# A transformer layer on one core: the first slots of the first stage in an order written out by hand, biases by two-row DMAs, identity products in TensorE's pauses

## The chip, the core and the metric

The kernel runs on one core of one Trainium2 chip. A core has TensorE (PE in the profile, PEld its weight loads), VectorE (DVE), ScalarE (ACT), GpSimd (POOL) and the sync engine (SP), which here only issues DMAs. Each engine works through its own queue in order; they meet through semaphores. Matrix products go to PSUM, which PE fills and DVE and ACT read. The metric is the time of one execution in device microseconds, as the median of several.

## The reference

One layer with a bidirectional retention branch, a grouped attention branch and a squared-ReLU MLP, on 2048 rows of width 1024 and 256 context rows. What the change touches is its beginning:

```python
mod = (c_act @ w_mod + b_mod)[:, None, :]
mod_c = (cc_act @ w_mod + b_mod)[None, None, :]
sh1, sc1, g1, sh2, sc2, g2 = jnp.split(mod, 6, axis=-1)
...
h = _modulate(_rmsnorm(x, norm1_g), sh1, sc1)        # h * (1 + scale) + shift
hc = _modulate(_rmsnorm(xc, norm1_g), csh1, csc1)
rq, rk, rv, rg, aq, ak, av = jnp.split(h @ w_in, SPLIT_IDX, axis=-1)
...
crk, crv = jnp.split(hc @ w_in[:, RK_OFF:RG_OFF], 2, axis=-1)
```

Then come rotary embedding, retention, attention over context and latent keys, the output product, the MLP and a last norm, all in float32.

## The kernel before

The layer runs in stages: the input projections (up to about 600 us), attention, the output product and the MLP. The projections are done in two groups of row tiles of 128: first the two context tiles c0, c1 with the latent tiles l0 to l3, then the other twelve. For each group the columns of `w_in` come in blocks, and a block of one tile is a *unit* or slot. Units follow one another on PE, and `run_step(s)` issues what else is due at unit s: loads, roundings of weights, evacuations, rotary embedding, stores. The table `do(s, part, fn)` is filled ahead with these, at distances in slots written out by hand. Engines see their instructions in the order in which the program issues them.

To keep float32 accuracy a product runs as three: the operand and the weights are each split into a rounded part (`hi`, by ACT) and the rest (`lo`, by DVE), and hi*hi, hi*lo and lo*hi are summed in one PSUM bank. That is the trio L1186, L1187 and L1188 of `products`.

The first block, the retention keys of the first six tiles (tiles 0 to 5 are c0, c1, l0 to l3), can't begin before the scale and shift of the norm are known, and these need the modulation. The function `start` therefore weaves both. Width 1024 is cut into quarters q of 256 columns. `Modulation(q)` loads its part of `w_mod` in four pieces (L340, two DMAs each), multiplies it on PE (L350, `product`), adds the bias (`end`, L353), turns the columns with an identity on PE (`columns`, L301) and takes sums to the shift `s1` and the scale `a1` (`shift_and_scale`, L360 to L363). `Rows` loads a tile of x, squares it (ACT, L460), takes the inverse root (POOL, L464 and L465) and scales the rows (DVE `norm`, L469); before, tiles go in pairs here. `Part(q, tile)` turns two 128-wide pieces of a tile (PE, L483), scales them (DVE, L488), adds the shift (POOL, L492), rounds (ACT `high`, L495) and takes the rest (DVE `low`, L498). `Weight` fetches and splits a quarter's two rows of key weights (L520, L526, L535).

*Round* q means the products of quarter q for tiles 0 to 4 (six a tile, `begun[n]` is the tile's bank); tile 5 has no bank until the end and runs all four quarters at once. Rounds 0 to 2 also carry the modulation of the next quarter. The list `order` in `start` is the order of the loads on the sync queue; `ahead` issues the next ones when one of six staging buffers (`wst`) has become free. Biases go out on ACT's queue, 32 rows of the same values each.

PSUM pools: `psM` one bank for the modulation's sums, `psT` two for turns, `psO` five for products.

Of the kernel before, what the change touches and what calls it, by code (L numbers as in the profile page):

```python
# [22 lines left out]
P = 128  # L23
# [33 lines left out]
def layer_kernel(ctx: ExitStack, tc: tile.TileContext, a: dict, out: bass.AP):  # L57
# [215 lines left out]
    with ExitStack() as st, tc.manual_schedule():  # L273
# [45 lines left out]
        class Modulation:  # L319
# [186 lines left out]
        class Weight:  # L506
# [8 lines left out]
            def fetch(self, j):  # L515
# [4 lines left out]
                nc.sync.dma_start(w, src.rearrange("(k p) n -> p k n", p=P))  # L520

# [679 lines left out]
        for (g, col), w in weights.items():  # L1201
# [93 lines left out]
        def start():  # L1295

            G, w0 = GROUPS[0], weights[0, C_RK]
            rows_ = mq.tile([P, 512], F32, name="mb", tag="mb", bufs=2)
            mods = [Modulation(q, rows_) for q in range(4)]
            rows = Rows(G, 2)  # L1300
            begun = {}
            for n in range(6):
                hs[0, n] = new_h(0, *G[n])
            order = [("m", 0, 0), ("x", 0), ("m", 0, 2), ("m", 0, 4), ("x", 1), ("m", 0, 6)]
            order += [("w", 0), ("x", 2), ("x", 3), ("m", 1, 0), ("x", 4), ("m", 1, 2), ("x", 5)]
            order += [("m", 1, 4), ("m", 1, 6), ("w", 1)]
            for q in (2, 3):
                order += [("m", q, k) for k in range(0, KT, 2)] + [("w", q)]
            room = [6]

            def ahead(n=1):
                room[0] += n
                while order and (order[0][0] == "x" or room[0]):
                    what, *at = order.pop(0)
                    if what == "x":
                        rows.load(*at)
                    elif what == "m":
                        room[0] -= 1
                        mods[at[0]].load(at[1])
                    else:  # L1320
                        room[0] -= 1
                        w0.fetch(*at)

            for m in mods[:2]:
                m.bias()
            nc.sync.dma_start(n1, a["n1"])
            ahead(0)

            def settle(*ns):
                for n in ns:  # L1330
                    rows.square(n)
                rows.root()
                for n in ns:
                    rows.norm(n)

            for k in range(0, KT, 2):
                mods[0].product(k)
                ahead()
            settle(0, 1)
            mods[0].end()  # L1340
            mods[0].shift_and_scale()
            w0.high(0)
            w0.low(0)
            ahead()
            parts = {}

            def begin(q, n):
                if q < 4 and n < 6:
                    p = parts[q, n] = Part(G[n][0], rows.x[n], hs[0, n], 2 * q, 2)
                    p.turn()  # L1350
                    p.scale()
                    p.shift()

            begin(0, 0)
            begin(0, 1)
            for q in range(4):
                for n in range(6):
                    parts[q, n].high()
                    parts[q, n].low()
                    if q == 0 and n == 2:  # L1360
                        settle(4, 5)
                    if q > 0 or n > 1:
                        begin(q, n + 2)
                    if n < 5:
                        if q == 0:
                            begun[n] = psO.tile([P, 512], F32, name="pso", tag="pso")
                        products(begun[n], hs[0, n], w0, 512, range(2 * q, 2 * q + 2))
                    elif q == 3:
# [1035 lines left out]
```

## Time and profile before

| | |
|---|---|
| time, median of 3 runs | 2692.89 us (2688.63 to 2694.88) |
| the profiled execution | 2693.04 us, span 2691.2 us, granted clock 0.997 |
| PE busy | 2618.1 us, 97% of the span |
| DVE, ACT, POOL busy | 2034.9, 1526.6 and 1729.1 us |
| first key product | 20.71 us |
| last product of the key block issued | 87.24 us |

A timeline row gives start, length, engine, line, instruction, what it writes and reads, how many were merged (x2), and in brackets how long the engine was idle before it and what ended that. Instructions on an engine are pipelined: a product of 0.39 us can follow another after 0.23. A float32 product that is not a turn has two records, so x16 of L350 are eight products. Names leave tile numbers out (`hhi_c` is the rounded part of c0 or c1). A row of a stretch gives the busy time of each engine in it.

### The profile page before, as it was taken

How to read it: one execution, taken by the hardware profiler on the slowest of the kernel's cores; microseconds unless marked ns; L12 is line 12 of the kernel's file. 1: busy time of each engine (PE TensorE's matmuls, PEld its weight loads, DVE VectorE, ACT ScalarE, POOL GpSimd, SP SyncE). 2: the span in 40 equal slices, each digit the busy share in tenths (PEclk: the TensorE clock that was granted, in tenths of full speed). 3: DMA queues.
4: the chain of work that ended last, by engine and by line, in shares of the span. 5: the costliest groups of instructions: out<-in, count | busy, mean ns of one | idle time of the engine just before them, and what ended most of it. 6: DMA issues, size and time to landing. Idle time of an engine off the chain costs nothing.

```text
span 2691.2 us, 45667 instructions
## 1 busy us (share of the span) xinstructions
PE 2618.1 (97%) x16759; PEld 1469.3 (55%) x16759; DVE 2034.9 (76%) x3032; ACT 1526.6 (57%) x2572; POOL 1729.1 (64%) x1351
## 2 busy tenths in 40 slices
PE   6999999998999999999999899999999999999998
PEld 3876555546666666666666444444444444444443
DVE  3688798677888888888887497989877566556686
ACT  2756444325877778788878576666666322222243
POOL 2545466545666668787787595777663566666686
PEclk9999999999999999999999999999999999999999
DMA  6766999746022113323332565666694857574453
GB/s 231 253 229 194 312 321 333 251 140 214 28 75 68 54 54 113 92 81 90 88 107 73 215 193 157 225 214 218 223 317 133 289 174 276 176 297 160 169 179 119
DMA packets 325065, 480.02 MB, mean 178 GB/s; under 512 B 82148, under 2 KB 192228, under 8 KB 320360
## 3 DMA queue, kind: packets, MB, share of 16 engines
q1 hardware_dynamic: 324456, 476.84, 53.4%
q8 instruction: 132, 2.16, 0.3%
q14 instruction: 93, 0.76, 0.1%
q10 hardware_dynamic: 384, 0.26, 0.0%
HBM read 320.03 MB, written 156.38 MB: 177 GB/s over the span
## 4 chain that ended last, share of the span: by engine, by line
PE 82%; DVE 8%; DMA 4%; ACT 3%; issue 2%; POOL 0%; SPq 0%; DVEq 0%; ACTq 0%; POOLq 0%
PE pd L2217 7%; PE pd L2216 7%; PE pd L2215 7%; PE pu L1988 7%; PE pu L1989 7%; PE pu L1990 7%; PE o L248 4%; PE st L214 4%; PE st L215 4%; PE pso L1188 4%; PE pso L1186 3%; PE pso L1187 3%; PE mp L177 3%; PE o L247 2%; PE bank L1757 2%; PE bank L1755 2%
## 5 line engine op out<-in xcount | busy, mean ns | idle before, releaser
L190 DVE TENSOR_REDUCE nm<-mp 128x1 f32<-128x512 f32 x558 | 379.2, 685 | 118.8 <-PE mp L177 103.6
L231 POOL TENSOR_TENSOR plo<-p,phi 128x1024 f16<-128x1024 f32 x160 | 346.1, 2164 | 157.5 <-ACT phi L224 136.0
L220 ACT ACTIVATE p<-st 128x512 f32<-128x512 f32 x576 | 340.4, 597 | 141.2 <-PE st L215 131.3
L1988 PE MATMUL pu<-hf,w1f 128*128 128x512 f16 x896 | 340.0, 379 | 0.0
L1989 PE MATMUL pu<-hf,w1f 128*128 128x512 f16 x896 | 339.8, 379 | 0.0
L1990 PE MATMUL pu<-hf,w1f 128*128 128x512 f16 x896 | 339.8, 379 | 0.0
L2215 PE MATMUL pd<-w,uf 128*128 128x512 f16 x896 | 339.6, 379 | 0.0
L2216 PE MATMUL pd<-w,uf 128*128 128x512 f16 x896 | 339.6, 379 | 0.0
L2217 PE MATMUL pd<-w,uf 128*128 128x512 f16 x896 | 339.6, 379 | 0.0
L2235 POOL TENSOR_TENSOR y<-y,d 128x512 f32<-128x512 f32 x128 | 210.4, 1646 | 147.5 <-ACT uf L2204 95.3
L224 ACT ACTIVATE phi<-p 128x1024 f16<-128x1024 f32 x288 | 303.8, 1055 | 0.0
L233 DVE TENSOR_TENSOR plo<-p,phi 128x512 f16<-128x512 f32 x256 | 235.9, 923 | 19.6 <-ACT phi L224 7.8
L248 PE MATMUL o<-wv,phi 128*128 128x129 f16 x2304 | 240.7, 220 | 0.0
L214 PE MATMUL st<-qr,ks 128*128 128x512 f16 x576 | 218.6, 380 | 14.9 <-ACT p L220 14.8
L247 PE MATMUL o<-wv,plo 128*128 128x65 f16 x2304 | 233.0, 193 | 0.0
L247 PEld LDWEIGHTS <-plo 128*128 128x128 f16 x2304 | 208.0, 98 | 22.0 <-issue 0.6
L215 PE MATMUL st<-qr,ks 128*128 128x512 f16 x576 | 218.5, 379 | 0.0
L248 PEld LDWEIGHTS <-phi 128*128 128x128 f16 x2304 | 205.2, 97 | 23.4
L2227 DVE SCALAR_TENSOR_TENSOR y<-pd,scy,y 128x512 f32<-128x512 f32 x160 | 116.9, 747 | 131.8 <-PE pd L2217 131.5
L2000 DVE TENSOR_TENSOR r<-pu,r 128x512 f32<-128x512 f32 x224 | 149.9, 684 | 83.3 <-PE pu L1990 59.5
L1186 PE MATMUL pso<-wf,h_l 128*128 128x512 f16 (+1 forms) x576 | 208.2, 361 | 0.0
L1188 PE MATMUL pso<-wf,h_l 128*128 128x512 f16 (+1 forms) x576 | 208.1, 361 | 0.0
(374 smaller groups left out, 6124.2 us busy)
## 6 DMA issues: line engine op xcount, KB each, us to landing
wm<-in_w_ff SPq DMA_DIRECT2D x64, 512.0 KB, 7.1
u<-r SPq DMA_DIRECT2D x128, 256.0 KB, 4.3
ur<-u SPq DMA_DIRECT2D x128, 256.0 KB, 5.5
y<-x SPq DMA_DIRECT2D x64, 512.0 KB, 6.9
wf<-w2f SPq DMA_DIRECT2D x112, 256.0 KB, 3.0
w<-wf SPq DMA_DIRECT2D x28, 1024.0 KB, 9.3
w1r<-in_w_ff SPq DMA_DIRECT2D x48, 512.0 KB, 4.9
x<-y SPq DMA_DIRECT2D x48, 512.0 KB, 2.9
```

Source lines behind the costliest of these rows:

```text
L190: nc.vector.tensor_reduce(dst, src, axis=AX.X, op=ALU.max, negate=True)
L214: mm(ps, ks[:, self.g, k], q[:, 0], start=True, stop=False)
L220: nc.scalar.activation(self.p[kt // 2][:, kt % 2], self.s.pop(kt), AF.Exp, scale=HD**-0.5)
L231: nc.gpsimd.tensor_tensor(lo, p, hi, op=ALU.subtract)
L247: mm(o[:, : HD + 1], lo[:, i, c], v[:, : HD + 1], start=False, stop=False)
L248: mm(o, hi[:, i, c], v[:, :VW], start=False, stop=last)
L1988: mm(pu[hf, i], whi, hi, start=k == 0, stop=False)
L1989: mm(pu[hf, i], whi, lo, start=False, stop=False)
L1990: mm(pu[hf, i], wlo, hi, start=False, stop=k == 3)
L2215: mm(ps, u[:, 0, b], w[:, b, 0], start=b == 0, stop=False)
L2216: mm(ps, u[:, 0, b], w[:, b, 1], start=False, stop=False)
L2217: mm(ps, u[:, 1, b], w[:, b, 0], start=False, stop=b == 3)
```

## The change

All in the first stage, in `start` and what it calls:

- Tiles are normed one by one (`Rows([t], 1)`), and the loads are ordered anew: the last modulation piece of quarter 0 ahead of tile 1, weights of quarters 2 and 3 ahead of the last piece of their modulation.
- The order of the first slots is written out. In round 0 each slot has the hi products of a tile, the turn and scaling of the next, the square and norm of the one after it, then the lo products and a piece of the next modulation. From the last tile of round 0 on, a slot has the hi products of its tile (`hi`, L1366 in the rows below), turns listed in `turns` for later slots, the split of what the slot before turned (`split_part`), and the lo products of the slot before (`lo`, L1371). A tile's `run_step` comes one slot later.
- `keep_on(n)` issues n products of the identity with itself (L1340) into the bank of tile 4 before that bank is used.
- Biases are two rows of each 32 (rows 0 and 16, the only ones that are read), in a buffer that POOL clears once at the start; those of quarters 2 and 3 go out on the sync queue.
- Weights of this block are split in two halves (`high_row`, `low_row`), and the columns are turned in the bank of `psM`.
- The weights of the attention queries (`C_AQ`) of the first group are fetched two slots and rounded one slot earlier.

The core of the diff:

```diff
-            def bias(self):
-                nc.gpsimd.memset(self.b[64:], 0.0)
+            def bias(self, queue):
...
-                    nc.scalar.dma_start(self.b[32 * i : 32 * i + 32], src.partition_broadcast(32))
+                    queue.dma_start(self.b[32 * i : 32 * i + 32 : 16], src.partition_broadcast(2))
...
-                ps = columns(self.b, 2, psT.tile([P, 4, P], F32, name="psx", tag="psx"))
+                ps = columns(self.b, 2, psM.tile([P, 4, P], F32, name="mps", tag="mps"))
...
+            def high_row(self, j, r):
...
+                nc.scalar.activation(self.w[j][0][:, r], self.raw[j][:, r], AF.Copy)
...
+                if (g, col) == (0, C_AQ):
+                    f, h = s - 7 + j, s - 4 + j
...
-            order = [("m", 0, 0), ("x", 0), ("m", 0, 2), ("m", 0, 4), ("x", 1), ("m", 0, 6)]
-            order += [("w", 0), ("x", 2), ("x", 3), ("m", 1, 0), ("x", 4), ("m", 1, 2), ("x", 5)]
-            order += [("m", 1, 4), ("m", 1, 6), ("w", 1)]
+            order = [("m", 0, 0), ("x", 0), ("m", 0, 2), ("m", 0, 4), ("m", 0, 6), ("w", 0), ("x", 1), ("x", 2)]
+            order += [("m", 1, 0), ("x", 3), ("m", 1, 2), ("x", 4), ("m", 1, 4), ("m", 1, 6), ("w", 1), ("x", 5)]
             for q in (2, 3):
-                order += [("m", q, k) for k in range(0, KT, 2)] + [("w", q)]
+                order += [("m", q, 0), ("m", q, 2), ("m", q, 4), ("w", q), ("m", q, 6)]
...
+            def keep_on(n):
+                for _ in range(n):
+                    mm(bank_of(4)[:, :P], ident, ident, start=True, stop=True)
...
+            keep_on(5)
+            add(0, 0)
+            square(0)
+            rows[0].norm(0)
+            keep_on(3)
+            add(0, 2)
+            keep_on(1)
+            add(0, 4)
+            turn(0, 0)
+            add(0, 6)
+            mods[0].end()
+            for r in range(2):
+                w0.high_row(0, r)
+            keep_on(1)
+            settled(0)
+            scale(0, 0)
+            for r in range(2):
+                w0.low_row(0, r)
...
+            keep_on(3)
+            parts[0, 0].high()
+            square(1)
+            parts[0, 0].low()
+            rows[1].norm(0)
+            for n in range(4):
+                hi(0, n)
+                if n == 0:
+                    keep_on(4)
+                turn(0, n + 1)
+                scale(0, n + 1)
+                if n < 3:
+                    square(n + 2)
+                parts[0, n + 1].high()
+                if n < 3:
+                    rows[n + 2].norm(0)
+                parts[0, n + 1].low()
+                lo(0, n)
+                add(1, 2 * n)
+                if n < 2:
+                    mods[2 + n].bias(nc.sync)
+                keep_on(2)
+            mods[1].end()
+            turn(1, 0)
+            settled(1)
+            scale(1, 0)
+            waiting = [(1, 0)]
+            turns = {(0, 4): [(1, 1), (1, 2)], (2, 2): [(0, 5), (1, 5)], (3, 2): [(2, 5)], (3, 3): [(3, 5)]}
+            for q in (1, 2, 3):
+                turns[q, 0], turns[q, 1] = [(q, 3)], [(q, 4)]
+                if q < 3:
+                    turns[q, 3], turns[q, 4] = [(q + 1, 0), (q + 1, 1)], [(q + 1, 2)]
+            pieces = {0: (0,), 1: (2,), 2: (4, 6)}
+            slots = [(0, 4)] + [(q, n) for q in (1, 2, 3) for n in range(5)]
+            for i, (q, n) in enumerate(slots):
+                ready, waiting = waiting, []
...
+                hi(q, n)
+                if n == 3 and q < 3:
+                    mods[q + 1].end()
+                    settled(q + 1)
+                for p in turns.get((q, n), ()):
+                    turn(*p)
+                    scale(*p)
+                    waiting.append(p)
+                for p in ready:
+                    split_part(*p)
...
+                if i:
+                    lo(*slots[i - 1])
+                if q in (1, 2):
+                    add(q + 1, *pieces.get(n, ()))
```

What this makes of PE's queue around the first key products. The names are `mps` for the modulation's bank, `psx` for turns, `pso` for a tile's bank, `x_c0` for tile 0 and so on, `hhi` and `hlo` for a part's rounded and remaining half; numbers are buffers. Before, from the last modulation piece of quarter 0:

```order
L350 MATMUL mps_393<-wst_379,cst_337 32x256 x4
L301 MATMUL psx_436<-ident_60,mb_346 128x128 x2
L483 MATMUL psx_449<-ident_60,x_c0_369 128x128 x2
L483 MATMUL psx_454<-ident_60,x_c1_377 128x128 x2
L1186 MATMUL pso_461<-whi_442,hhi_c0_347 128x512
L1187 MATMUL pso_461<-wlo_443,hhi_c0_347 128x512
L1188 MATMUL pso_461<-whi_442,hlo_c0_348 128x512
```

And now, at the same place and on into the second slot:

```order
L482 MATMUL psx_434<-ident_60,x_c0_370 128x128 x2
L349 MATMUL mps_398<-wst_378,cst_337 32x256 x4
L1340 MATMUL pso_392<-ident_60 128x128
L301 MATMUL mps_452<-ident_60,mb_346 128x128 x2
L1340 MATMUL pso_392<-ident_60 128x128 x3
L1366 MATMUL pso_478<-whi_446,hhi_c0_348 128x512
L1366 MATMUL pso_478<-wlo_447,hhi_c0_348 128x512
L1366 MATMUL pso_478<-whi_446,hhi_c0_348 128x512
L1366 MATMUL pso_478<-wlo_447,hhi_c0_348 128x512
L1340 MATMUL pso_392<-ident_60 128x128 x4
L482 MATMUL psx_487<-ident_60,x_c1_383 128x128 x2
L1371 MATMUL pso_478<-whi_446,hlo_c0_349 128x512 x2
```

Tile 0's turn now stands ahead of the last modulation piece and tile 1's behind the first products; lo products follow a slot's hi products, and identity products (L1340) fill in.

DVE's queue in the same stretch, before, from the first norms:

```order
L469 TENSOR_SCALAR x_c_369<-x_c_369,xy 128x1024
L469 TENSOR_SCALAR x_c_377<-x_c_377,xy 128x1024
L353 TENSOR_TENSOR mb<-mps,mb 128x256
L360 TENSOR_REDUCE s_274<-psx 128x2x2
L360 TENSOR_REDUCE sc<-psx 128x4
L363 SCALAR_TENSOR_TENSOR a_273<-sc,n_341 128x2x2
L535 TENSOR_TENSOR wlo<-wst,whi 128x1024
L488 TENSOR_TENSOR x_c_369<-psx,a_273 128x256
```

And now:

```order
L468 TENSOR_SCALAR x_c0_370<-x_c0_370,xy_412 128x1024
L352 TENSOR_TENSOR mb_346<-mps_398,mb_346 128x256
L359 TENSOR_REDUCE s1_274<-mps_452 128x2x2
L359 TENSOR_REDUCE sc_451<-mps_452 128x4
L362 SCALAR_TENSOR_TENSOR a1_273<-sc_451,n1_341 128x2x2
L487 TENSOR_TENSOR x_c0_370<-psx_434,a1_273 128x256
L528 TENSOR_TENSOR wlo_447<-wst_381,whi_446 128x512 x2
L497 TENSOR_TENSOR hlo_c0_349<-x_c0_370,hhi_c0_348 128x256
L468 TENSOR_SCALAR x_c1_383<-x_c1_383,xy_473 128x1024
L487 TENSOR_TENSOR x_c1_383<-psx_487,a1_273 128x256
L468 TENSOR_SCALAR x_l0_385<-x_l0_385,xy_496 128x1024
L497 TENSOR_TENSOR hlo_c1_351<-x_c1_383,hhi_c1_350 128x256
```

The second norm has left the place ahead of the bias sum (L353, now L352), the scaling stands ahead of the weights' low half, and from then on a norm stands ahead of each low half.

PE in round 1, tiles 0 and 1. Before:

```order
L1186 MATMUL pso_461<-whi_559,hhi_c0_347 128x512
L1187 MATMUL pso_461<-wlo_560,hhi_c0_347 128x512
L1188 MATMUL pso_461<-whi_559,hlo_c0_348 128x512
L1186 MATMUL pso_461<-whi_559,hhi_c0_347 128x512
L1187 MATMUL pso_461<-wlo_560,hhi_c0_347 128x512
L1188 MATMUL pso_461<-whi_559,hlo_c0_348 128x512
L350 MATMUL mps_617<-wst_446,cst_337 32x256 x4
L350 MATMUL mps_617<-wst_503,cst_337 32x256 x4
L483 MATMUL psx_634<-ident_60,x_l1_386 128x128 x2
```

And now, from tile 1's slot:

```order
L1366 MATMUL pso_516<-whi_615,hhi_c1_350 128x512
L1366 MATMUL pso_516<-wlo_616,hhi_c1_350 128x512
L1366 MATMUL pso_516<-whi_615,hhi_c1_350 128x512
L1366 MATMUL pso_516<-wlo_616,hhi_c1_350 128x512
L482 MATMUL psx_667<-ident_60,x_l2_406 128x128 x2
L1371 MATMUL pso_478<-whi_615,hlo_c0_349 128x512 x2
L349 MATMUL mps_655<-wst_509,cst_337 32x256 x4
```

The lo products of tile 0 stand behind the hi products of tile 1, and the turn between them belongs to tile 4, three slots on.

More of the change, by code (lines that the diff above doesn't have):

```diff
@@ new lines, in keep_on, with add, square, turn @@
+            def keep_on(n):
+                for _ in range(n):
+                    mm(bank_of(4)[:, :P], ident, ident, start=True, stop=True)
+            def add(q, *ks):
+                for k in ks:
+                    mods[q].product(k)
+                    ahead()
+            def square(n):
+                rows[n].square(0)
+                rows[n].root()
+            def turn(q, n):
+                p = parts[q, n] = Part(G[n][0], rows[n].x[0], hs[0, n], 2 * q, 2)
+                p.turn()
@@ L1324, in start, with settled @@
+            def settled(q):
+                mods[q].shift_and_scale()
+            for r in rows_:
+                nc.gpsimd.memset(r, 0.0)
             for m in mods[:2]:
-                m.bias()
+                m.bias(nc.scalar)
             nc.sync.dma_start(n1, a["n1"])
             ahead(0)
[L1329 to L1338, printed above, removed]
```

118 lines of the change are left out of this document (58 added, 60 removed).

## The prediction

> **What bounds the kernel now.** I read the page first, then the busy time by stretch, then the timeline of the first 90 us instruction by instruction, then the waits there. The page says that TensorE is the bound, with little to take away:
>
> ```profile
> span 2691.2 us, 45667 instructions
> PE 2618.1 (97%) x16759; PEld 1469.3 (55%) x16759; DVE 2034.9 (76%) x3032; ACT 1526.6 (57%) x2572; POOL 1729.1 (64%) x1351
> ```
>
> The stretches show where the missing 3% lie. The columns are the stretch, its length, then busy us of PE, PEld, DVE, ACT and POOL, the granted clock, the DMA share and GB/s:
>
> ```profile
> 0.00:20.71 20.71, 8.25 (x39) 2.54 (x39) 4.35 (x13) 5.27 (x8) 3.31 (x13) 1.00 0.87 298
> 20.71:38.52 17.81, 12.96 (x69) 9.21 (x69) 7.91 (x17) 6.98 (x14) 4.60 (x10) 0.90 0.85 288
> 38.52:87.47 48.95, 39.56 (x226) 26.64 (x225) 28.95 (x64) 14.97 (x30) 17.27 (x25) 1.00 0.40 125
> 35.00:85.00 50.00, 39.30 (x224) 26.16 (x223) 28.80 (x68) 15.06 (x30) 15.82 (x25) 1.00 0.37 114
> 87.47:200.00 112.53, 109.24 (x583) 91.59 (x582) 80.14 (x132) 76.20 (x140) 56.37 (x72) 1.00 0.77 267
> ```
>
> Of the kernel's 73 us without a busy PE, 26.7 lie ahead of 87.47, where the retention keys (the first block) end. That is the stretch which the change writes anew. Behind it PE lacks 3.3 us in 112. So the question is how much earlier than 87.47 us that block ends, and whether the rest follows. I count three steps: until the first key product (20.71), through the first fifth of the block to the last tile of round 0 (38.52), and from there on.
>
> **Step 1, until the first product.** The rows of the chain into it:
>
> ```profile
> 12.79 1.06 ACT L460 ACTIVATE junk<-x_c 128x1024 bf16<-128x1024 f32 x1 [2.52 <-DMA x_c<-in_ctx]
> 14.08 0.19 PEld L350 LDWEIGHTS mps<-wst,cst 128*32 128x32 f32 x4 [0.50 <-DMA wst<-in_w_mod]
> 14.03 0.19 POOL L464 TENSOR_SCALAR xv<-ss 128x2 f32<-128x2 f32 x1 [12.08 <-ACT junk L460]
> 15.06 1.42 DVE L469 TENSOR_SCALAR x_c<-x_c,xy 128x1024 f32<-128x1024 f32 x2 [12.02 <-POOL xy L465]
> 16.39 0.42 DVE L353 TENSOR_TENSOR mb<-mps,mb 128x256 f32<-128x256 f32 x1
> 16.91 0.66 PE L301 MATMUL psx<-ident,mb 128*128 128x128 f32 x2 [1.76 <-issue]
> 17.60 0.17 DVE L360 TENSOR_REDUCE s<-psx 128x4 f32<-128x8 f32 x1 [0.80 <-PE psx L301]
> 17.95 1.23 DVE L535 TENSOR_TENSOR wlo<-wst,whi 128x1024 fp32r<-128x1024 f32 x1
> 19.09 0.75 DVE L488 TENSOR_TENSOR x_c<-psx,a 128x256 f32<-128x256 f32 x2
> 19.59 1.18 POOL L492 TENSOR_TENSOR x_c<-x_c,s 128x256 f32<-128x256 f32 x2 [4.57 <-DVE x_c L488]
> 20.24 0.42 ACT L495 ACTIVATE hhi_c<-x_c 128x256 fp32r<-128x256 f32 x1 [3.36 <-POOL x_c L492]
> 20.71 0.80 PE L1186 MATMUL pso<-whi,hhi_c 128*128 128x512 f32 x1 [2.06 <-ACT hhi_c L495]
> ```
>
> The last modulation weights land at 14.08, fifth in the transfers' order behind tile 1 of x, which landed at 12.79. The change swaps these two, all lie in one saturated queue (share 0.87), so I let the weights land at tile 1's place in the bytes, 12.8. The sum with the bias (L353) then need not wait: before, it stood on DVE behind two norms (15.06 plus 1.42). In the new order only tile 0 is normed ahead of it, long before. From landing to the end of the products PE takes 13.40 plus 1.75 less 14.08, so 1.07:
>
> ```profile
> 13.40 1.75 PE L350 MATMUL mps<-wst,cst 128*32 128x256 f32 x8 [0.82 <-DMA wst<-in_w_mod]
> ```
>
> That gives 13.87. The sum 0.42: 14.3. The turn of the columns until the first reduction 0.69 (16.91 to 17.60): 15.0. Reductions 0.35 (17.60 to 17.95): 15.35. There the low halves of the weights, 1.23 us of DVE, step behind the scaling. Scaling to shift 0.50, shift to rounding 0.65, rounding to product 0.47: **17.0**, 3.7 us before 20.71.
>
> **Step 2, round 0.** Here the change works on one tile at a time. In a slot ScalarE squares the tile after next, POOL takes its root behind the shift of the next tile, DVE norms it, PE turns it, DVE scales it. The rows behind the prices:
>
> ```profile
> 38.38 0.38 PE L483 MATMUL psx<-ident,x_c 128*128 128x128 f32 x2
> 38.52 0.49 PE L1186 MATMUL pso<-whi,hhi_l 128*128 128x512 f32 x1
> 38.80 0.42 DVE L488 TENSOR_TENSOR x_c<-psx,a 128x256 f32<-128x256 f32 x1 [1.17 <-PE psx L483]
> 39.30 0.72 POOL L492 TENSOR_TENSOR x_c<-x_c,s 128x256 f32<-128x256 f32 x1 [0.91 <-DVE x_c L488]
> 43.74 1.07 PE L350 MATMUL mps<-wst,cst 128*32 128x256 f32 x16
> 44.75 0.44 PE L483 MATMUL psx<-ident,x_l 128*128 128x128 f32 x2
> ```
>
> Rounding of tile 0 starts at 16.5 by step 1, so the square of tile 1 at 16.8. From square to root 1.24 (12.79 to 14.03), root to norm 1.03 (14.03 to 15.06), norm 0.75 and 0.05 to PE, turn to scaling 0.42, scaling to shift 0.50: the shift of tile 1 starts at 20.8. From one shift to the next it is 0.65 plus 1.03, 0.8, 0.42 and 0.50, so 3.4 us, since POOL and DVE take these steps in this order and the squares (1.24) fit beside them. Tile 4's shift starts at 31.0. Then 0.65, rounding 0.42, low half 0.42 (as a scaling, the same size), the modulation's sum 0.47 and the columns 0.22: the last tile's products begin at **33.2** instead of 38.52, 5.3 us earlier. PE has 2.55 us of work in such a slot (six products at 0.23, two turns 0.22, a modulation pair 0.5 as half of 43.74 to 44.75, two identity products), so it isn't the bound there.
>
> What I price at nothing in these two steps: 25 identity products. No row shows one; the nearest is a product of the same shape and type, 0.225 (four in 423.68 to 424.58):
>
> ```profile
> 423.68 1.06 PE L1154 MATMUL psf<-early 128*128 128x128 f32 x8
> 424.58 0.38 PE L1186 MATMUL pso<-wf,h_l 128*128 128x512 f16 x1
> ```
>
> All stand where PE waits for DVE, POOL, ScalarE or a landing; uncovered they cost 5.6 us, twice that at half clock. A gain from them I bound below, under the clock. Biases by two rows: the old ones land 3.7 us after issue, and an issue on the sync queue takes 0.44:
>
> ```profile
> mb<-in_b_mod ACTq DMA_DIRECT2D x8, 32.0 KB, 3.7
> 9.11 0.88 SPq L340 DMA_DIRECT2D wst<-in_w_mod  x2
> ```
>
> A sixteenth of the bytes should land no later, and is due some 10 us after issue. On the sync queue four of them stand ahead of the key weights of quarter 2. These follow the third modulation product of round 0 (about 28 by step 2) and are rounded in the fourth slot of round 1, about 41, so 1.8 us of issues are hidden; if that cover is gone, they cost 1.8. The weights' rounding and low half in two halves cost ScalarE and DVE one more instruction each, beside PE's products. Two larger memsets stand ahead of the identity on POOL, whose first use that matters is the turn of tile 0, near 12. The columns' turn in the modulation's bank makes the next modulation products wait for three reductions, and these products come at least one slot later.
>
> **The clock.** The 0.23 us product is seen only from 25.09 on:
>
> ```profile
> 24.29 0.63 PE L1188 MATMUL pso<-whi,hlo_c 128*128 128x512 f32 x1
> 24.71 0.54 PE L1186 MATMUL pso<-whi,hhi_c 128*128 128x512 f32 x1
> 25.09 0.39 PE L1187 MATMUL pso<-wlo,hhi_c 128*128 128x512 f32 x1
> 25.32 0.40 PE L1188 MATMUL pso<-whi,hlo_c 128*128 128x512 f32 x1
> 32.00:33.00 1.00, 1.00 (x4) 0.82 (x3) 0.70 (x2) 0.00 (x0) 0.10 (x1) 0.50 0.98 296
> ```
>
> Before that, and again at 32 where the granted clock is 0.50, a product takes 0.42. Fifteen such products cost 3 us, which lie inside the 20.71 to 38.52 that step 2 replaces; that is the most that the identity products can bring by themselves. In the new order the stretch from 17.0 is dense (four products, four identity products, about 3.4 us at half clock), and no pause after it is over 1 us, so I take full clock from the second slot. The Trainium skill (TensorE: Matmul & The Clock Gate, Part 1 and "A second HAM failure mode") says that the clock doubles after about 3.4 us of activity, but also that frequent small pauses between groups can make it swing back; the first agrees with 20.71 to 24.71, the second no row here shows. Part 4 adds that turns do not count as activity. By that second rule the time is that of the first rival below.
>
> **Step 3, from the last tile of round 0.** Before, rounds 1 and 3 begin 29.5 us apart, so a round lasts 14.7:
>
> ```profile
> 40.99 0.48 PE L1186 MATMUL pso<-whi,hhi_c 128*128 128x512 f32 x1
> 70.46 0.48 PE L1186 MATMUL pso<-whi,hhi_c 128*128 128x512 f32 x1
> PE pso L1188 <- DVE hlo_l L498: 7.9, 7, 2.4
> ```
>
> PE's own work from 38.52 to 87.47 is 120 products at 0.23 (27.6), eight modulation pairs at 0.5 (4.0), 17 pairs of turns at 0.22 (3.7) and two columns (0.4): 35.8 of 48.95 us, so 13.1 are waits (the busy column counts a product's whole flight of 0.39 and so shows 9.4), and the last row names their kind: the third product of a trio waits for the low half. The change gives PE the high products of a slot first and the low ones of the slot before, and turns a part two slots ahead of its use. From a turn to the rounded part are 2.0 us (0.42, 0.50, 0.65, 0.42), to its low half 2.4. Slots now hold 1.6 to 2.6 us of PE work; between a turn and the high products that need it lie the rest of one slot and the whole of another, and the low ones come one slot later still. What still waits: the columns at the start of round 1 (reductions, scaling, shift and rounding 2.0 us against 1.36 of PE work) and the low weights at each round's first slot; I put 1.5 us for these, with 0 and 5 as ends. So 33.2 plus 36.0 (one more pair of turns) plus 1.5 is **70.7** instead of 87.47: 16.8 us.
>
> **Behind the block.** Weights, tables and stores are tied to slots, so they move with PE. The queues have room: from 35 to 85 the DMA share is 0.37, and 50 x 0.63 is 31 us, more than the 17 given up. The attention queries have their weights fetched two slots and rounded one slot earlier; PE didn't wait for them before, since its 3.3 us of waits up to 200 are these:
>
> ```profile
> 180.37 0.66 PE L705 MATMUL psx<-ident,ys 128*128 128x128 f32 x4 [1.29 <-DVE x_l L488]
> 195.99 1.06 PE L483 MATMUL psx<-ident,x_l 128*128 128x128 f32 x8 [1.99 <-DVE x_l L469]
> ```
>
> So I take nothing for that edit, and the shift whole.
>
> **The rivals.** (1) *Round 0 stays at half clock.* A slot is then 4.85 us of PE work (products 0.42, the rest doubled) against 3.4: 4 x 1.45 is 5.8 us, 2682.0. For it: pauses of 0.85 us in each slot; against it: four dense microseconds sufficed before. Chance 0.10. (2) *Half of it is given back* on DVE, which is busy 80 of 112 us behind the block and makes PE wait there: 2684.6. Against it: DVE's work there starts from landings and from PE, both earlier. Chance 0.08. (3) *The loop isn't broken:* on DVE's queue a tile's low half stands behind the scaling of a freshly turned one, which stands behind PE's high products, which wait for a rounding. If this closes, a slot lasts as long as round 0's 3.4: 33.2 plus 16 x 3.4 plus 5.5 for tile 5 is 93.1, 5.6 us later than before, 2698.6. It decides from 3.05 us per slot, where the time is that of before; the old loop ran at 2.9 (14.7 by five), so this isn't far. Against it: the lead just counted. Chance 0.10, over half of it slower. The forecast has 0.72.
>
> **The numbers.** The profiled execution took 2693.04 us, 1.84 beside its span; the median of three is 2692.89, so they are one and the same. 2693.04 less 16.8 is 2676.2. The forecast's own range is 2671 (no waits left, the 3.3 us behind the block gone too) to 2680 (5 us of waits). With the first two rivals it ends at 2686. A difference of 0.2% (5.4 us) is about what can be told from none. Faster are the forecast and the first two rivals, 0.90 less 0.01 for a larger loss on DVE; the third is slower with 0.07, and the same 0.04 are the rest.
>
> **What would show it.** First key product near 17, last tile of round 0 near 33, end of the block near 71, products at 0.23 from about 21 on. Product waits for low halves gone in rounds 1 to 3. Wrong if slots of rounds 1 to 3 last 3 us, if products of round 0 stay at 0.42, or if the block ends by 71 and PE's waits up to 200 us have grown from 3.3 us.

## The result, and the profile after

The changed kernel takes 2678.56 us (median of 4, 2678.08 to 2681.22) beside 2692.15 of before: a ratio of 0.9948, 95% interval 0.9936 to 0.9961, so 13.6 us less. Five later executions of it gave 0.9955 (0.9942 to 0.9969). The profiled execution took 2678.23, its span is 2676.4:

```profile
span 2676.4 us, 45775 instructions
PE 2621.9 (98%) x16809; PEld 1472.1 (55%) x16809; DVE 2036.6 (76%) x3036; ACT 1526.4 (57%) x2576; POOL 1735.1 (65%) x1355
```

The busy time by stretch of the changed kernel, cut at its own first key product (17.18), last tile of round 0 (33.17), end of the key block (74.08) and first turn of attention keys (100.43; columns as in the prediction):

```profile
0.00:17.18 17.18, 10.72 (x62) 6.12 (x62) 3.22 (x11) 4.15 (x8) 3.00 (x12) 0.90 0.79 254
17.18:33.17 15.99, 14.54 (x93) 8.79 (x93) 7.28 (x15) 6.93 (x14) 5.41 (x12) 1.00 1.01 357
33.17:74.08 40.91, 38.99 (x227) 27.09 (x226) 29.48 (x68) 16.41 (x34) 18.86 (x25) 1.00 0.51 160
74.08:100.43 26.35, 25.04 (x186) 23.37 (x184) 15.15 (x25) 19.53 (x42) 14.20 (x20) 1.00 0.96 325
```

The last of these stretches in the kernel before, which the prediction did not cut out:

```profile
87.47:112.08 24.61, 24.61 (x185) 23.38 (x184) 10.69 (x21) 19.62 (x43) 10.08 (x18) 1.00 0.96 328
```

PE's waits from the last tile of round 0 to the end of round 3, of before and then of after. Columns: engine, tile and line, what it waited for; total, number and longest in us:

```profile
PE pso L1188 <- DVE hlo_l L498: 6.6, 6, 2.4
PE pso L1188 <- DVE hlo_c L498: 2.7, 3, 0.9
```

```profile
PE pso L1366 <- ACT hhi_c L494: 1.0, 1, 1.0
PE pso L1366 <- DVE wlo L528: 0.8, 2, 0.7
PE mps L301 <- DVE mb L352: 0.5, 1, 0.5
```

No wait for a tile's low half is left there; `wlo` is the low half of weights, and the wait for `mb` ends just before the last tile's products. The two spans differ by 14.80 us, and five differences make up all but 0.1 of that: 3.53 until the first product (20.71 to 17.18), 1.82 in round 0 (17.81 to 15.99), 8.04 in the rest of the block (48.95 to 40.91), 1.74 lost in the stretch behind it (24.61 to 26.35), and 3.05 at one wait near the kernel's middle, which the change doesn't touch. In the 14 profiles of this case that wait takes 0.97 to 4.39 us (1.65 in the kernel before with two loads swapped, 4.18 in the changed kernel with one weight rounded earlier), so its size here is chance. Its rows, before and after:

```profile
1544.02 1.94 PE L1787 MATMUL bank<-ident,xr 128*128 128x128 f32 x8 [4.36 <-DVE u L1792]
```

```profile
1530.76 1.23 PE L1870 MATMUL bank<-ident,xr 128*128 128x128 f32 x8 [1.31 <-DVE u L1875]
```

What remains without it, 11.75 us, is the change. The medians' 13.6 and 12.1 (2692.62 x 0.0045) agree with that within their intervals.

### The profile page after: what moved, and what is told of

It is laid out like the page before. It is cut to its first block, busy times and chain, and to the rows that moved or that the text cites. A ratio compares the mean times of both kernels' runs of the same rounds, so it can differ in the third digit from the quotient of the medians.

```text
span 2676.4 us, 45775 instructions
## 1 busy us (share of the span) xinstructions
PE 2621.9 (98%) x16809; PEld 1472.1 (55%) x16809; DVE 2036.6 (76%) x3036; ACT 1526.4 (57%) x2576; POOL 1735.1 (65%) x1355
## 4 chain that ended last, share of the span: by engine, by line
PE 83%; DVE 7%; ACT 4%; DMA 4%; issue 2%; SPq 0%; POOL 0%; ACTq 0%; DVEq 0%; POOLq 0%
PE pd L2300 7%; PE pd L2299 7%; PE pd L2298 7%; PE pu L2072 7%; PE pu L2073 7%; PE pu L2071 7%; PE o L248 4%; PE st L214 4%; PE st L215 4%; PE pso L1194 4%; PE pso L1195 4%; PE pso L1196 3%; PE mp L177 3%; PE o L247 2%; PE bank L1840 2%; PE bank L1839 2%
## 5 line engine op out<-in xcount | busy, mean ns | idle before, releaser
L214 PE MATMUL st<-qr,ks 128*128 128x512 f16 x576 | 218.6, 379 | 14.9 <-ACT p L220 14.8
```

## The experiments

All were timed beside the kernel before; the last runs of the list draw on what the first showed. *First* is the first key product, *last tile* the last tile of round 0, *end* the end of the key block, *behind* the length of the stretch from there to the first turn of attention keys; all from the profiled executions, us.

| kernel | median | ratio (95%) | first | last tile | end | behind |
|---|---|---|---|---|---|---|
| before | 2692.15 | 1 | 20.71 | 38.52 | 87.47 | 24.61 |
| changed | 2678.56 | 0.9948 (0.9936 to 0.9961) | 17.18 | 33.17 | 74.08 | 26.35 |
| changed again | 2681.26 | 0.9955 (0.9942 to 0.9969) | 17.10 | 33.08 | 74.00 | 26.07 |
| no identity products | 2682.92 | 0.9961 (0.9949 to 0.9974) | 17.75 | 34.93 | 75.84 | 25.60 |
| old discipline in rounds 1 to 3 | 2689.15 | 0.9983 (0.9975 to 0.9992) | 17.53 | 34.17 | 82.36 | 25.61 |
| low products in own slot | 2683.44 | 0.9966 (0.9954 to 0.9978) | 17.64 | 33.62 | 76.37 | 25.87 |
| old query-weight slots | 2685.39 | 0.9971 (0.9962 to 0.9981) | 17.52 | 33.91 | 74.82 | 29.54 |
| turns a slot earlier | 2678.13 | 0.9942 (0.9930 to 0.9955) | 16.41 | 31.22 | 72.11 | 26.01 |
| last query weight earlier | 2680.02 | 0.9951 (0.9938 to 0.9963) | 16.82 | 32.79 | 73.72 | 24.48 |
| before, two loads swapped | 2697.61 | 1.0014 (1.0005 to 1.0023) | 24.44 | 41.92 | 90.44 | 24.47 |
| both earlier | 2678.03 | 0.9943 (0.9930 to 0.9955) | 18.07 | 32.89 | 73.76 | 24.48 |
| with squares earlier too | 2676.32 | 0.9936 (0.9922 to 0.9949) | 17.64 | 30.90 | 70.67 | 24.47 |
| old biases | 2684.23 | 0.9966 (0.9954 to 0.9979) | 18.51 | 36.76 | 77.67 | 26.30 |
| old load order | 2682.63 | 0.9966 (0.9953 to 0.9978) | 20.17 | 36.17 | 77.05 | 24.49 |

Ratios of neighbours overlap; where an edit is worth 1 to 3 us the verdict comes from the positions. These are of one execution each and scatter too: in six profiles whose instructions are the same up to the first product (changed, changed again, and the runs on rounds 1 to 3, on low products and on query weights, old and earlier) the first product lies at 16.82 to 17.64, and in the three with turns ahead at 16.41 to 18.07.

**Rounds 1 to 3.** The slots' rounding and low products put back where they are used:

```diff
+                if q:
+                    split_part(q, n)
                 hi(q, n)
+                lo(q, n)
...
-                    split_part(*p)
+                    if p[1] == 5:
+                        split_part(*p)
...
-                if i:
-                    lo(*slots[i - 1])
```

> The changed kernel, but in rounds 1 to 3 a tile's rounding and its low half are issued again in the slot that uses them, and its low products directly behind its high ones, as before the change; turns stay where the change put them. If the lead and lag are what took the waits for low halves away, the waits of before come back: 9.3 us in rounds 1 to 3 of before against 1.8 now, so about 7.5 us more, 2686. If the gain of these rounds comes from elsewhere (turns two slots ahead, weights rounded in halves, the earlier start), it loses 1.5 us at most, 2678.5 to 2680.

Round 1's first product to the block's end takes 45.43 us (36.93 to 82.36) instead of 38.16 (35.92 to 74.08): 7.3 more, close to the price expected, and the waits of that stretch are of the old kind again:

```profile
PE pso L1371 <- DVE hlo_l L497: 4.7, 2, 2.4
PE pso L1366 <- ACT hhi_l L494: 1.0, 2, 0.8
PE pso L1366 <- ACT hhi_c L494: 0.7, 1, 0.7
```

With one of 0.2 they sum to 6.6 us. The wait of 0.7 ends where the stretch begins, so 5.9 lie in it, 5.1 more than the changed kernel's 0.8. The other 2.1 us are no wait: in this execution 3.4 us at half clock fell into round 3 (from 65.75). So the waits by themselves are under the 7.5 expected. In the kernel before, 9.3 us were waited from the last tile of round 0 on; what keeps the rest away here, the turns two slots ahead or another part of the change, no run takes out by itself. Which of the two, lead or lag, takes the 5.1 away? Only the low products put back:

```diff
                 hi(q, n)
+                lo(q, n)
...
-                if i:
-                    lo(*slots[i - 1])
```

> The changed kernel, only with the low products of rounds 1 to 3 in their own slot, behind the high ones; rounding and low half stay one slot ahead. If the lead of the rounding is the active part, low halves are ready and it costs 0 to 1.5 us, 2678.5 to 2680. If the lag of the low products is, most of the 7.5 us of the run before it shows: 2682 to 2686.

39.99 us for the same stretch, 1.8 more than the changed kernel, 1.1 of it waits: a little over the first expectation. The time, 2683.44, lies in the second's range, but its ratio overlaps the changed kernel's. By the positions, the rounding one slot ahead carries about 4 of the 5.1 us, the lag of the low products the rest.

**The identity products** (`keep_on` issues nothing):

```diff
-                for _ in range(n):
-                    mm(bank_of(4)[:, :P], ident, ident, start=True, stop=True)
+                pass
```

> The changed kernel (2678.56 us) without its identity products, nothing else. If they are worth what the clock theory says, the first key products fall back to 0.42 us as they did before the change (at 20.7 to 24.7 us): up to 16 products of round 0 at 0.19 us more each, so up to 3 us, about 2680 to 2681.5, with the first key product still near 17.2. If they are cover for nothing, round 0 keeps its 3.4 us slots, which POOL and DVE set, and the time is 2678 to 2679; if they even stood in the way, up to 1 us less, 2677.5.

The block ends 1.76 us later, 0.57 of it ahead of the first product, most of which is within the scatter, and 1.19 in round 0. Of round 0's rows these are the second tile's products, 0.43 apart, and then the stretch, with a granted clock of 0.80 where the changed kernel has 1.00:

```profile
23.58 0.63 PE L1365 MATMUL pso<-wlo,hhi_c 128*128 128x512 f32 x1
24.00 0.63 PE L1365 MATMUL pso<-whi,hhi_c 128*128 128x512 f32 x1
24.43 0.63 PE L1365 MATMUL pso<-wlo,hhi_c 128*128 128x512 f32 x1
17.75:34.93 17.18, 13.47 (x68) 7.04 (x69) 7.46 (x16) 6.92 (x14) 5.40 (x12) 0.80 0.99 354
```

The 6.8 us at half clock from 18.98 on lie in round 0 here. With identity products the half clock took none of round 0 (changed, changed again) or 3.4 us of it (in the runs on rounds 1 to 3 and with the old query weights, where round 0 lasts 16.6 and 16.4 us). The block ends at 73.7 to 74.8 in the four profiles that have them with the new loop, loads and biases (74.82 with the old query weights), so in this one execution they would be worth 1.0 to 2.1 us, below the bound of 3; that it comes through the clock fits the rows, and how much of it is chance stays open.

**The loss behind the block.** The old slots for the attention queries' weights:

```diff
-                if (g, col) == (0, C_AQ):
-                    f, h = s - 7 + j, s - 4 + j
```

> The changed kernel with the attention queries' weights fetched and rounded at the slots of before. New in the trace after the change is a loss of 1.74 us at 97 to 99 us, where the last of these weights is rounded late. If ScalarE's queue is jammed by copies that wait for stores in the full transfer queue, the old timing puts two roundings behind that jam and costs 1 to 3 us more, 2679.5 to 2681.5. If the new timing itself caused the loss, it goes: 2676.8.

The stretch behind takes 29.54 us, 3.2 to 3.5 more than in the changed kernel's two profiles: PE waits 2.9 us there instead of 1.3 and 1.1, and behind the longest of these waits (2.1) its clock is halved for a while (granted 0.94 over the stretch). The edit that the prediction took nothing for earns that; it isn't the cause of the loss. What is, the changed kernel's rows show: ScalarE's copy `zs` waits for the store of an earlier one, and behind it on the queue stands the rounding of the fourth weight, which PE needs (ScalarE, then PE):

```profile
95.26 0.60 ACT L742 ACTIVATE zs<-psx 128x512 f32<-128x512 f32 x1 [3.94 <-DMA kt<-zs]
95.75 1.05 ACT L936 ACTIVATE junk<-wm 128x1024 bf16<-128x1024 f32 x1
96.79 1.05 ACT L534 ACTIVATE whi<-wst 128x1024 fp32r<-128x1024 f32 x1
...
97.89 0.50 PE L1194 MATMUL pso<-whi,hhi_l 128*128 128x512 f32 x1 [0.55 <-ACT whi L534]
99.15 0.50 PE L1195 MATMUL pso<-wlo,hhi_l 128*128 128x512 f32 x1 [0.76 <-DVE wlo L543]
```

Rounding that weight one slot earlier should then mend it:

```diff
-                    f, h = s - 7 + j, s - 4 + j
+                    f, h = s - 7 + j, min(s - 4 + j, s - 2)
```

> The changed kernel with the last of the attention queries' four weights rounded one slot earlier, with the third. If its rounding stands on ScalarE's queue behind a copy that waits for a store (1.74 us lost at 97 to 99 us), the loss goes and the stretch from the end of the key block to the first turn of keys falls from 26.35 to about 24.6 us: 1.0 to 1.7 us less than the changed kernel. If the weights' landing is what is late, the stretch stays at 26.3.

It does. The weight is rounded at 86.49 with the third (`x2`), the copy still waits 3.06, and PE is busy all of the stretch:

```profile
86.49 2.01 ACT L534 ACTIVATE whi<-wst 128x1024 fp32r<-128x1024 f32 x2
...
94.85 0.60 ACT L742 ACTIVATE zs<-psx 128x512 f32<-128x512 f32 x1 [3.06 <-DMA kt<-zs]
...
73.72:98.20 24.48, 24.48 (x185) 23.46 (x184) 16.56 (x28) 19.08 (x40) 15.68 (x26) 1.00 0.95 325
```

**The loads.** The swap alone, in the kernel before, and the swap undone in the changed kernel:

```diff
-            ... ("m", 0, 4), ("x", 1), ("m", 0, 6)]
+            ... ("m", 0, 4), ("m", 0, 6), ("x", 1)]
```

> The kernel before, with only the order of two transfers swapped: the last modulation weights ahead of tile 1 of x. If the swap by itself brought the first key product forward, it begins at 17 to 18 instead of 20.71 and about 3 us are saved. By step 1 it does not: tiles 0 and 1 are normed together, so tile 1, now landing last at about 14.1, holds up both norms on DVE and the modulation's sum behind them, and the first key product comes at 20.7 to 22.0, 0 to 1.3 us more than before.

The direction is that of step 1, the size isn't: 3.7 us later. The norms of the pair hold up the sum as expected, but tile 1 lands at 16.47 and not at 14.1; why so late no run shows. The rows are its square, the norms, the sum and the first product:

```profile
16.47 1.06 ACT L460 ACTIVATE junk<-x_c 128x1024 bf16<-128x1024 f32 x1 [6.15 <-DMA x_c<-in_ctx]
...
18.74 1.42 DVE L469 TENSOR_SCALAR x_c<-x_c,xy 128x1024 f32<-128x1024 f32 x2 [15.66 <-ACT whi L526]
20.07 0.42 DVE L353 TENSOR_TENSOR mb<-mps,mb 128x256 f32<-128x256 f32 x1
...
24.44 0.79 PE L1186 MATMUL pso<-whi,hhi_c 128*128 128x512 f32 x1 [2.06 <-ACT hhi_c L495]
```

```diff
-            order = [... ("m", 0, 4), ("m", 0, 6), ("w", 0), ("x", 1), ("x", 2)]
+            order = [... ("m", 0, 4), ("x", 1), ("m", 0, 6), ("w", 0), ("x", 2)]
```

> The changed kernel with tile 1 of x loaded ahead of the last modulation weights, as before. By step 1 the weights then land a tile later, near 14.1 instead of 12.9, and the first key product moves with them: 18.3 to 18.5 instead of 17.2, and 1.0 to 1.3 us more in time. If the landing of the first key weights is what sets it (their rounding waited for a landing until 15.68 in the changed kernel), they too come a tile later and the product moves by the same; if neither, it stays at 17.2.

The last weights' products start at 14.85 instead of 12.90 (after's rows are the second pair), and the first key product comes at 20.17, 3.0 later rather than 1.3:

```profile
14.85 1.61 PE L349 MATMUL mps<-wst,cst 128*32 128x256 f32 x8 [2.04 <-DMA wst<-in_w_mod]
15.54 0.14 PEld L349 LDWEIGHTS mps<-wst,cst 128*32 128x32 f32 x4 [0.55 <-DMA wst<-in_w_mod]
```

```profile
12.90 0.93 PE L349 MATMUL mps<-wst,cst 128*32 128x256 f32 x8
13.21 0.14 PEld L349 LDWEIGHTS mps<-wst,cst 128*32 128x32 f32 x4 [0.16 <-DMA wst<-in_w_mod]
```

The weight loads show when the second half of this piece lands: 2.3 us later. From there the products take 0.92 us and not 0.62, since half clock is granted from 15.75 on; the remaining 0.4 us lie in the chain behind them. So landing makes most of the 3 us. At the first key product the swap costs 3.7 us where tiles are normed in pairs and earns 2 to 3, given the scatter, where they are normed one at a time.

**The biases** as 32 rows each, all on ScalarE's queue, at the places of the changed kernel:

```diff
-                    queue.dma_start(self.b[32 * i : 32 * i + 32 : 16], src.partition_broadcast(2))
+                    nc.scalar.dma_start(self.b[32 * i : 32 * i + 32], src.partition_broadcast(32))
```

> The changed kernel with the biases fetched as before, as 32 rows each and all from ScalarE's queue. By step 2 of the prediction the two-row form was priced at nothing: the biases are due some 10 us after their issue and land in under 4. The same time as the changed kernel, within 0.5 us, and the same positions in the key block. If the 15/16 of their bytes that the change takes away, or the issues on ScalarE's queue in front of roundings, matter in the full transfer queue, the first key product or the last tile of round 0 comes 0.5 to 2 us later.

The first expectation failed. Round 0 lasts 18.25 us (18.51 to 36.76) instead of 15.99, and a new wait stands in it (ScalarE's queue, ScalarE, PE):

```profile
30.35 0.32 ACTq L332 DMA_DIRECT2D mb<-in_b_mod  x1
30.71 1.06 ACT L459 ACTIVATE junk<-x_l 128x1024 bf16<-128x1024 f32 x1 [3.66 <-DMA mb<-in_b_mod]
...
32.22 0.50 PE L1366 MATMUL pso<-whi,hhi_l 128*128 128x512 f32 x1 [1.59 <-ACT hhi_l L494]
```

The bias of quarter 3 waits for the landing of quarter 2's, which fills the same tile, and ScalarE waits with it while a square and a rounding stand behind. On the sync queue only loads wait. The slot with this wait lasts 5.1 us instead of 3.4, which is 1.7 of round 0's 2.3; the first slot, 0.5 longer, has 3.4 us at half clock. The 1.3 us that the first product comes later are not shown to be the biases': 6.8 us at half clock fell on the modulation here, as in a run with the new biases below whose first product came at 18.07. The edit changes rows and queue together, and the wait speaks for the queue; what 32 rows cost by themselves is not shown.

**Better than both?** Step 2 said that round 0's slots are set by the chain shift, root, norm, turn and scaling. Then a turn one slot earlier shortens them:

```diff
+            square(2)
+            hi(0, 0)
+            keep_on(4)
+            turn(0, 1)
+            scale(0, 1)
+            rows[2].norm(0)
             for n in range(4):
-                hi(0, n)
...
-                turn(0, n + 1)
-                scale(0, n + 1)
...
                 parts[0, n + 1].high()
-                if n < 3:
-                    rows[n + 2].norm(0)
+                if n < 2:
+                    square(n + 3)
...
-                keep_on(2)
+                if n < 3:
+                    turn(0, n + 2)
+                    scale(0, n + 2)
+                if n < 2:
+                    rows[n + 3].norm(0)
+                if n < 3:
+                    hi(0, n + 1)
```

> The changed kernel with round 0's turns, norms and squares of a tile one slot earlier, and without the identity products between those slots. If the chain shift, root, norm, turn, scaling over POOL and DVE sets the 3.4 us slots (step 2 of the prediction), they fall to TensorE's own 2.2 to 2.8 us, and the last tile of round 0 begins 2 to 3 us earlier, near 31: about 2.5 us less than the changed kernel. If the transfers set them (the DMA share is 1.03 to 1.09 from 17 to 30 us), nothing is gained: the same time, within 0.5 us.

Last tile at 31.22, 1.95 earlier, but 0.77 of that is scatter ahead of the first product (16.41). In round 0 it is 1.2: the third and the last slot fall from 3.4 and 4.4 us to 3.0, and the first grows from 4.9 to 5.5, with 3.4 us at half clock in it. That is more than the 2.2 to 2.8 a slot that was expected. The transfers are as full as in the changed kernel (DMA share 1.01 in both), so they don't set the slots. With the query weight's edit added:

> The two edits of the last runs together: round 0's turns one slot earlier without identity products between its slots, and the last of the attention queries' weights rounded with the third. In the profiles they moved the end of the key block from 74.0 to 72.1 us and shortened the stretch behind it from 26.1 to 24.5 us. If the two are independent, the sum shows: first turn of keys at about 96.5 us, 3.5 us less than the changed kernel, near 2676. If the transfer queue behind the block, already full from 75 to 95 us, takes it back, the stretch grows again to about 26 us and the time is that of the first edit alone, 2678.

The stretch behind stays at 24.48, so the transfer queue takes nothing back; round 0 lasts 14.8 us in both. The first product came at 18.07 in this execution, which hides the sum in the positions, and the time, 2678.03 at a ratio of 0.9943, is that of the first edit alone: no time shows the sum of 2676 that was expected. Then squares ahead too, round 0's last low products into the wait at round 1's start, tile 5's rounding behind the weights' low halves (against the run before this one):

```diff
+                if n < 2:
+                    square(n + 3)
                 parts[0, n + 1].high()
-                if n < 2:
-                    square(n + 3)
...
-                    split_part(*p)
+                    if p[1] == 5 and n == 3 and q < 3:
+                        waiting.append(p)
+                    else:
+                        split_part(*p)
...
-                if i:
-                    lo(*slots[i - 1])
+                if i != 1:
+                    lo(*slots[max(i - 1, 0)])
```

> The same with three more edits in the key block: in round 0 the squares of a tile are issued ahead of the rounding of the tile before, so that root and norm come earlier; the low products of round 0's last tile fill the 1.0 us wait at the start of round 1; tile 5's rounding steps behind the weights' low halves (0.7 us wait at 60 us). If round 0's slots are still set by the norm (waits of 0.9 and 0.6 us for it in the run with turns ahead), they fall to about 2.5 us and with the other two waits the block ends 2.5 to 3 us earlier than in the run above, near 69.5 us, and the time is near 2673.5. If the transfers hold round 0, its slots stay at 3.0 us and only 1.2 us are gained.

From the second tile to the fourth, round 0's high products now start 2.4 us apart:

```profile
23.18 0.50 PE L1366 MATMUL pso<-whi,hhi_c 128*128 128x512 f32 x1 [0.19 <-ACT hhi_c L494]
...
25.56 0.50 PE L1366 MATMUL pso<-whi,hhi_l 128*128 128x512 f32 x1
...
27.93 0.50 PE L1366 MATMUL pso<-whi,hhi_l 128*128 128x512 f32 x1
```

The block ends at 70.67, though its first product was 0.5 us later than the changed kernel's, and the time is 2676.32 (2674.97 to 2677.01). The block's end moved by the 3 us expected, the time by 1.7 and not to 2673.5. All five lie below the fastest of the changed kernel's nine, 2678.08. By ratio to before, 0.9936, it is the fastest here, though its interval overlaps the changed kernel's.

The changed kernel itself beside these:

> The changed kernel itself once more, beside the other three on one chip. Its ratio to before was 0.9948 (0.9936 to 0.9961); the forecast's mechanism and every rival expect the same again, with the start of the block behind the keys at 74 to 75 us. What is open is the spread: whether the stretches of 3.4 us at half clock fall elsewhere in this execution than at 9.0, 616, 630 and 1497 us.

Positions agree within 0.1 us up to 93 us. Then they part: the stretches behind are those of the section on the hardware.

## Why the prediction was right, and where its sum was off

The forecast was 2676.2 in 2670 to 2686; the profiled execution took 2678.23, the median is 2678.56. Its steps:

- **Step 1** gave 17.0; 17.18, and in part by luck. The last weights were due at 12.8; the load that waits for them starts at 13.21 (shown above), 0.4 later. From there the products end 0.6 us on and not 1.07, which was a price at half clock, so the chain goes on at 13.83 as forecast (13.87). Not seen was that the key weights' landing (rounded from 15.68) ends at the same time as the chain through the shift. Other executions of the same instructions gave 16.82 to 17.64.
- **Step 2** gave 33.2; 33.17. The shifts of tiles 1 and 4 were put at 20.8 and 31.0, with 3.4 from one tile's to the next:

```profile
20.91 0.61 POOL L491 TENSOR_TENSOR x_c<-x_c,s 128x256 f32<-128x256 f32 x1 [1.82 <-DVE x_c L487]
...
24.26 0.61 POOL L491 TENSOR_TENSOR x_l<-x_l,s 128x256 f32<-128x256 f32 x1 [1.82 <-DVE x_l L487]
...
31.07 0.61 POOL L491 TENSOR_TENSOR x_l<-x_l,s 128x256 f32<-128x256 f32 x1 [1.89 <-DVE x_l L487]
```

  The chain is the one forecast, and breaking it shortened the slots. That it hit to 0.03 us is luck: where half clock fell into round 0's first slot, the round lasted 0.4 to 0.7 us longer.

- **Step 3** is the term that was mis-sized: 36.0 of work and 1.5 of waits were forecast, so 37.5, and 40.91 came. The waits are 1.8, but the work is 39.1. The mistake is the clause that put 120 products at 0.23 and set aside the busy column because it "shows a product's whole flight". In these rounds a product takes 0.23 from its start to the next start only behind another of its kind; the first after a turn, a modulation product or a wait takes 0.31 to 0.34, as the starts of the first three show:

```profile
17.18 0.50 PE L1366 MATMUL pso<-whi,hhi_c 128*128 128x512 f32 x1 [1.71 <-ACT hhi_c L494]
17.52 0.40 PE L1366 MATMUL pso<-wlo,hhi_c 128*128 128x512 f32 x1
17.76 0.40 PE L1366 MATMUL pso<-whi,hhi_c 128*128 128x512 f32 x1
```

  From one start to the next, the 120 products take 31.2 us here (0.26 each), 3.6 more than the 27.6 forecast; the other work is 0.5 less. The busy column of before said 39.56 of 48.95 and the waits' view 9.3: both were right (so 9.3 and not 13.1 were waits before), and with them step 3 would have been 33.2 plus 39.6 plus 1.5, 74.3, against 74.08.
- **Behind the block** the shift was to stay whole. 1.74 us were given back, as in the second rival, but on ScalarE behind a store and not on DVE. This too was a sentence without a row: "PE didn't wait for them before" speaks of a slot in which the copy's wait had 0.92 us of room (the copy started 0.92 us ahead of the queries' first product, 105.55 to 106.47; after, 2.19 behind it, 95.26 to 93.07).
- 2676.2 plus 3.4 plus 1.7, less the 3.05 of chance at 1531 us and 0.1, is the profiled time. Without that chance it would be 2681.2, still in the range but past 2680, the end of the forecast's own; the nearness to 2676.2 is luck.
- **The rivals.** The loop is broken, as forecast: waits of over 2 us for low halves came back only in the run that restored the old discipline. The first rival's half clock did come in round 0, for one stretch, in some executions (below). Biases and query weights, both at nothing in the sum, are worth about 1.7 and 3 us against their old forms: "hidden" was right for what the change put there and wrong for what it took away.

## What to carry to other kernels

Take a block's work from the start-to-start times between waits, or from the busy column, not from the shortest spacing times a count; every change of kind in front of a matrix product cost about 0.1 us here. When a block moves forward, look for the in-order queue on which something urgent stands behind something that waits for a transfer, since the transfers need not move as far: here the queries' first product came 13.4 us earlier, the copy's start behind its store 10.3. An operation that lands in time can still be dear by the queue that it is issued from.

## What the hardware showed unexpectedly

TensorE's half clock comes in pieces of 3.4 us or a multiple (up to 10.2 in these profiles, the very end of the kernel aside), and where they fall differs between executions of the same instructions. In the two profiles of the changed kernel PE waits 1.99 us for the same norm (from 182.6 and 182.3 us). The first goes on at full clock, the second doesn't:

```profile
182.00:186.00 4.00, 2.01 (x14) 1.50 (x13) 4.00 (x6) 1.22 (x3) 3.00 (x3) 1.00 0.00 0
186.00:190.00 4.00, 4.00 (x19) 3.32 (x18) 4.00 (x5) 4.00 (x8) 3.58 (x4) 1.00 0.56 163
```

```profile
182.00:186.00 4.00, 2.01 (x12) 1.62 (x11) 4.00 (x5) 1.54 (x3) 3.26 (x4) 0.86 0.00 0
186.00:190.00 4.00, 4.00 (x14) 3.20 (x13) 4.00 (x6) 4.00 (x8) 3.62 (x4) 0.71 0.66 190
```

0.14 and 0.29 of 4 us, doubled, are 3.4 us at half clock, and the stretch from the first turn of attention keys (100.43 and 100.07) to the first product of the second group (210.01 and 211.30) takes 109.58 and 111.23: 1.65 us by chance. Such a piece follows this wait in 8 of the 14 profiles of this case. The same holds at the start: with the same instructions up to round 0, the piece lay before the first key product in some profiles (at 8.99 and 9.03 us, for example) and in round 0's first slot in others (at 17.97 and 18.27). The Trainium skill (TensorE: Matmul & The Clock Gate, Part 1) has a window of 3413 ns that runs freely, not reset by a kernel's start; that agrees with the size and the scatter. What the Trainium skill says of frequent small pauses between groups of products (the same page, "A second HAM failure mode"), the prediction's first rival, no run here isolates; what the traces show is the piece behind a single pause of 2 us.

The granted clock of a stretch is not to be trusted ahead of its first recorded change, which in the kernel before comes at 25.02 us. It shows 1.00 here, where its products stand 0.42 us apart (the prediction's rows at 24.29 and 24.71):

```profile
20.71:25.09 4.38, 4.38 (x10) 3.47 (x11) 1.35 (x3) 2.61 (x5) 0.97 (x3) 1.00 1.07 394
```
